# Key norms of a linear-attention mixer: squares as the stationary side, tokens on partitions

## The chip, the cores and the metric

The kernel runs on one core of one Trainium2 chip. The metric is the device time of one execution in microseconds (us); lower is better. The core's engines are named as in the profile: PE is TensorE (matrix products; PEld is its load of the stationary side), DVE is VectorE, ACT is ScalarE, POOL is GpSimd, and SP is SyncE, which here issues nearly all DMAs.

## The reference, cut to what matters

One residual block over 512 tokens of width 1024: a gated feed-forward, a mixer, a second gated feed-forward, each between two normalisations. The mixer has two halves: a delta-rule time mixing with 8 heads of 64 channels, and a causal convolution of width 31 over 512 channels. The change lies in the first half, in the sum over a head's 64 channels of the squared scaled key:

```python
r, k, v = ps[..., :o1], ps[..., o1:o2], ps[..., o2:o3]
...
kk = heads(k * k_k)
kk = kk * lax.rsqrt(jnp.maximum(jnp.sum(kk * kk, axis=-1, keepdims=True), 1e-12))
...
y = rwkv7_recurrence(rh, wh, kh, vh, -kk, kk * ah)
```

Per token t and head, the recurrence updates a state S by S = S (diag(w_t) + z_t^T b_t) + v_t^T k_t, with z_t = -kk_t, b_t = kk_t a_t, and reads y_t = S r_t.

## The kernel before, in words

Inputs, outputs and intermediate results are float32. Large products are made of three passes in a split format: each operand is cut into a high and a low part (`whi`, `wlo` for weights, `hT` for activations), and `mm3` issues high by high (L129), low by high (L132) and high by low (L133). Weights come as blocks of 128 x 1024 by DMA on SP's queue (`wraw`), ACT rounds them to the high part (L105), DVE subtracts to get the low part (L108).

The program runs the first feed-forward (0 to 385 us of the trace), the mixer (385 to 663) and the second feed-forward (663 to 1053). In the mixer the heads are handled as four pairs, two heads of 64 channels on the 128 partitions, 512 tokens along the free dimension. For each pair `prep` makes one projection of 24 matmuls for the key (`psk`), one for `r` and one for `v`, with much in between:

- decay and rate from small up-projections (matmuls L723 and L725), scans and exponentials on DVE and ACT;
- the arrays `bk` (two scaled keys, last written at L747) and `z`;
- the key norm (L751 to L757): ACT squares the scaled key into a tile `sq` (its tag is `tk`), PE sums over channels with two columns of ones (`ind`, a view of the tile `blkones`), ACT copies the sum out of PSUM (L755), and a DMA writes it to the DRAM tensor `nd` (L756);
- the score matrices in `scores`: 16 matmuls L799, 16 L807 and 64 L817 per pair, each 64 partitions deep, with masked copies out of PSUM (`ZT` at L803, `LU` at L823, `E` at L830 or L828);
- the centred values (L778, L779) copied to `SV` by ACT (L780, L781), and the bonus matmul L783, whose PSUM buffer those copies free.

Two pairs make a group. `solve(G)` writes the group's score matrices to DRAM (`md` from `Mt`, L840), reads them back in another layout (`N`, L845, and `D`, the norms from `nd`, L846), takes the reciprocal of `D`, multiplies `N` by it (L853) and solves 31 steps of a triangular system on DVE (L862, L865). Results go out and back through DRAM (`rd`, `td`, into `Mt` and `T`), and `solve_b` takes them up on PE (L903). The tokens of `nd` stand in rows of 64 (pair, chunk of 64 tokens, head, half chunk) with 32 tokens each.

The convolution of a channel block waits for two projections, then makes its padded input `gpad` (L663, DVE); some of its tokens are summed on DVE (L671, L674), the rest by products on ACT (L678, L681) and sums on POOL (L682).

What stands next to what on an engine's queue is not written out: a list scheduler orders every engine's instructions by priorities and by its own model of durations and dependencies. The string `PLAN` and the tables `O_*` and `T_*` set priorities and the tags of PSUM buffers (tags A and B have three buffers each, C has two). A small change in one operation can therefore reorder what follows it on any engine.

Of the kernel before, what the change touches and what calls it, by code (L numbers as in the profile page):

```python
# [18 lines left out]
P = 128  # L19
D = 1024  # L20
SEQ = 512
# [505 lines left out]
T_PR = 'BBBBC'  # L527
# [13 lines left out]
class Mixer:  # L541
# [160 lines left out]
    def prep(self, hp):  # L702
        c, nc, v = self.c, self.c.nc, self.v
        G, l = hp // 2, hp % 2
# [9 lines left out]
        gr = (slice(0, 64), slice(64, 128))  # L714
        for par in range(2):
# [33 lines left out]
        nc.vector.scalar_tensor_tensor(z, ch(k), v["k_k"][:, h1], lam[:, :, 0:64], ALU.mult, ALU.mult)  # L749
        sq = self.t([P, SEQ], "tk", 2)  # L750
        nc.scalar.activation(sq, k, AF.Square, scale=v["k_k"][:, h1])  # L751
        pn = self.ps([2, SEQ], T_PR[1])
        nc.tensor.matmul(pn, lhsT=self.ind, rhs=sq, start=True, stop=True)
        n2 = sq[0:2]
        nc.scalar.copy(n2, pn)  # L755
        nc.sync.dma_start(self.ndram[G].rearrange("(l c h f) i -> l h c (f i)", l=2, c=8, h=2)[l],  # L756
                          n2.rearrange("h (c i) -> h c i", c=8))  # L757
        tc.cur_priority += O_PR[hp] - O_PK[hp]
        psr = self.proj()
        r_ = self.t([P, SEQ], "tk", 2)  # L760
# [559 lines left out]
```

## Time and profile before

| what | us |
|---|---|
| median of 2 runs (1056.44 to 1057.47) | 1056.95 |
| the profiled execution | 1054.72 |
| its span in the trace | 1052.9 |
| PE busy | 1011.4 (96%) |
| DVE busy | 777.1 (74%) |
| ACT busy | 484.8 (46%) |
| POOL busy | 147.0 (14%) |

The profiled execution is one of its own, 1.8 us of it outside the span. Times of views are counted from the span's start. A busy PE is not a PE at its best pace: matmuls overlap in their pipeline, so the pace is read from the distance between starts, not from one row's duration. A float32 matmul outside the split format shows as two passes (x2).

### The profile page before, as it was taken

How to read it: one execution, taken by the hardware profiler on the slowest of the kernel's cores; microseconds unless marked ns; L12 is line 12 of the kernel's file. 1: busy time of each engine (PE TensorE's matmuls, PEld its weight loads, DVE VectorE, ACT ScalarE, POOL GpSimd, SP SyncE). 2: the span in 40 equal slices, each digit the busy share in tenths (PEclk: the TensorE clock that was granted, in tenths of full speed). 3: DMA queues.
4: the chain of work that ended last, by engine and by line, in shares of the span. 5: the costliest groups of instructions: out<-in, count | busy, mean ns of one | idle time of the engine just before them, and what ended most of it. 6: DMA issues, size and time to landing. Idle time of an engine off the chain costs nothing.

```text
span 1052.9 us, 18597 instructions
## 1 busy us (share of the span) xinstructions
PE 1011.4 (96%) x7570; PEld 892.1 (85%) x7570; DVE 777.1 (74%) x1392; ACT 484.8 (46%) x724; POOL 147.0 (14%) x164
## 2 busy tenths in 40 slices
PE   8999999999999899989988898999999999999997
PEld 8899999998888787757667676788999999988885
DVE  5799989985334756789568797687999899853335
ACT  7453444443224435665766375433534444432232
POOL 0000000000000020365788380000000000000000
PEclk9999999999999999999996989999999999999999
DMA  5233333324425221212420310722333333234231
GB/s 200 81 121 104 117 101 107 100 96 145 150 89 185 86 81 62 77 56 80 91 72 22 61 62 5 271 86 82 120 103 118 101 107 100 96 131 144 89 118 80
DMA packets 54589, 107.77 MB, mean 102 GB/s; under 512 B 28776, under 2 KB 28904, under 8 KB 54504
## 3 DMA queue, kind: packets, MB, share of 16 engines
q1 hardware_dynamic: 53640, 103.96, 30.9%
q10 hardware_dynamic: 864, 2.63, 0.7%
q8 instruction: 59, 0.97, 0.4%
q14 instruction: 26, 0.21, 0.1%
HBM read 98.69 MB, written 7.88 MB: 101 GB/s over the span
## 4 chain that ended last, share of the span: by engine, by line
PE 81%; DVE 10%; ACT 3%; DMA 3%; issue 1%; POOL 1%; SPq 0%; DVEq 0%; ACTq 0%; POOLq 0%
PE ps L129 25%; PE ps L133 25%; PE ps L132 25%; DVE ps L674 1%; DVE wlo L108 1%; PE ps L941 1%; PE ps L817 1%; DMA lraw<-w 1%; POOL cacc L682 1%; DMA D<-nd 1%; DVE E L945 1%; ACT cacc L1033 1%; PE ps L194 1%; DVE llo L108 0%; ACT whi L105 0%
## 5 line engine op out<-in xcount | busy, mean ns | idle before, releaser
L108 DVE TENSOR_TENSOR wlo<-wraw,whi 128x1024 fp32r<-128x1024 f32 x103 | 129.2, 1254 | 138.2 <-ACT whi L105 137.8
L129 PE MATMUL ps<-hT,whi 128*128 128x256 f32 (+1 forms) x600 | 196.2, 329 | 1.1 <-ACT hT L179 0.7
L105 ACT CAST whi<-wraw 128x1024 fp32r<-128x1024 f32 x105 | 110.2, 1050 | 184.9 <-PE ps L132 107.5
L133 PE MATMUL ps<-hT,whi 128*128 128x256 f32 (+1 forms) x600 | 194.4, 326 | 0.4 <-DVE hT L186 0.2
L132 PE MATMUL ps<-hT,wlo 128*128 128x256 f32 (+1 forms) x600 | 194.2, 325 | 0.3 <-DVE ms_s L164 0.3
L682 POOL TENSOR_TENSOR cacc<-cacc,cpr 128x512 f32<-128x512 f32 (+2 forms) x120 | 128.6, 1071 | 33.3 <-ACT cpr L681 25.0
L129 PEld LDWEIGHTS ps<-hT,whi 128*128 128x128 f32 x600 | 114.9, 192 | 14.8 <-issue 3.1
L133 PEld LDWEIGHTS ps<-hT,whi 128*128 128x128 f32 x600 | 114.4, 191 | 11.8 <-issue 1.7
L132 PEld LDWEIGHTS ps<-hT,wlo 128*128 128x128 f32 x600 | 115.0, 192 | 10.4 <-issue 1.5
L132 PE MATMUL ps<-whi,gh 128*128 128x512 f32 x288 | 112.0, 389 | 0.0
L133 PE MATMUL ps<-wlo,gh 128*128 128x512 f32 x288 | 112.0, 389 | 0.0
L681 ACT ACTIVATE cpr<-gpad,vecs 128x512 f32<-128x512 f32 (+2 forms) x120 | 71.1, 601 | 37.4 <-POOL cacc L682 37.0
L132 PE MATMUL ps<-tsum,slo 128*128 128x256 f32 x288 | 80.0, 283 | 0.0
L133 PE MATMUL ps<-tsum,shi 128*128 128x256 f32 x288 | 80.0, 283 | 0.0
L129 PE MATMUL ps<-tsum,shi 128*128 128x256 f32 x288 | 76.3, 283 | 0.0
L129 PE MATMUL ps<-whi,gh 128*128 128x512 f32 x288 | 71.5, 389 | 0.0
L133 PEld LDWEIGHTS ps<-wlo,gh 128*128 128x128 f32 x288 | 54.1, 188 | 11.2
L132 PEld LDWEIGHTS ps<-whi,gh 128*128 128x128 f32 x288 | 54.1, 188 | 11.2
L129 PEld LDWEIGHTS ps<-whi,gh 128*128 128x128 f32 x288 | 53.9, 188 | 11.1
L132 PEld LDWEIGHTS ps<-tsum,slo 128*128 128x128 f32 x288 | 55.3, 192 | 0.0
L133 PEld LDWEIGHTS ps<-tsum,shi 128*128 128x128 f32 x288 | 55.3, 192 | 0.0
L365 ACT CAST shi<-s 128x1024 fp32r<-128x1024 f32 x36 | 37.8, 1050 | 36.0 <-DVE s L358 22.1
(273 smaller groups left out, 2328.0 us busy)
## 6 DMA issues: line engine op xcount, KB each, us to landing
wraw<-w SPq DMA_DIRECT2D x105, 512.0 KB, 3.6
lraw<-w SPq DMA_DIRECT2D x57, 512.0 KB, 3.7
x<-x SPq DMA_DIRECT2D x8, 512.0 KB, 4.5
xs<-x SPq DMA_DIRECT2D x8, 512.0 KB, 2.6
x<-xs SPq DMA_DIRECT2D x8, 512.0 KB, 6.3
gain<-gains ACTq DMA_DIRECT2D x5, 512.0 KB, 5.2
out<-x SPq DMA_DIRECT2D x3, 512.0 KB, 2.6
N<-md SPq DMA_DIRECT2D x4, 256.0 KB, 3.6
```

The lines of the kernel that those rows point to most:

```text
L105: c.last_hi = nc.scalar.copy(hi, raw)
L108: c.last_lo = (eng or nc.vector).tensor_tensor(lo, raw, hi, ALU.subtract)
L129: i = nc.tensor.matmul(out, lhsT=lh, rhs=rh, start=start, stop=False)
L132: nc.tensor.matmul(out, lhsT=ll, rhs=rh, start=False, stop=False)
L133: return nc.tensor.matmul(out, lhsT=lh, rhs=rl, start=False, stop=stop)
L194: i = c.nc.tensor.transpose(out=pt[:, k], in_=self.xn[t][:, kk * P : (kk + 1) * P], identity=c.ident)
L365: nc.scalar.copy(sh, sums)
L674: self.dve_queue(nc.vector.scalar_tensor_tensor(dst, gp[:, j : j + n], dw[:, j : j + 1], lo, ALU.mult, ALU.add), False)
L681: nc.scalar.mul(pr, gp[:, n + j : j + SEQ], dw[:, j : j + 1])
L682: self.pool_queue(nc.gpsimd.tensor_tensor(hi, hi, pr, ALU.add), j == 1)
L817: nc.tensor.matmul(ps[s][dst[par], cc, r], lhsT=bk[g, c0 + cc, s], rhs=E[g, l, par, c0 + cc, 1] if r else I2[g], start=True, stop=True)
L941: nc.tensor.matmul(pa[par][:, cc].rearrange("p a b -> p (a b)"), lhsT=Z_[g, d0 + cc].rearrange("p a b -> p (a b)"), rhs=L_[g, d0 + cc].rea ...
```

## The change

Before, the ones are the stationary side (128 x 2) and the squares the moving side (128 x 512), so the sum comes out as 2 partitions (heads) by 512 tokens, and one DMA writes it to `nd` in 16 runs of 64 tokens.

After, each block of 128 tokens of the squares is the stationary side and the two columns of ones move: four matmuls per pair, whose sums come out as 128 partitions (tokens) by 4 blocks by 2 heads. ACT copies them to a new tile `n2` of 128 x 8, and four DMAs write them, one for each half of the partitions (`a`) and head (`h`), with 64 x 4 single elements of 4 bytes each. The content of `nd` is the same.

```diff
         sq = self.t([P, SEQ], "tk", 2)
         nc.scalar.activation(sq, k, AF.Square, scale=v["k_k"][:, h1])
-        pn = self.ps([2, SEQ], T_PR[1])
-        nc.tensor.matmul(pn, lhsT=self.ind, rhs=sq, start=True, stop=True)
-        n2 = sq[0:2]
+        pn = self.ps([P, 4, 2], T_PR[1])
+        for t in range(4):
+            nc.tensor.matmul(pn[:, t], lhsT=sq[:, t * P : t * P + P], rhs=self.ind, start=True, stop=True)
+        n2 = self.t([P, 4, 2], "n2")
         nc.scalar.copy(n2, pn)
-        nc.sync.dma_start(self.ndram[G].rearrange("(l c h f) i -> l h c (f i)", l=2, c=8, h=2)[l],
-                          n2.rearrange("h (c i) -> h c i", c=8))
+        nd = self.ndram[G].rearrange("(l t a h f) i -> l a h (f i) t", l=2, t=4, a=2, h=2)[l]
+        for a in range(2):
+            for h in range(2):
+                nc.sync.dma_start(nd[a, h], n2[gr[a], :, h])
         tc.cur_priority += O_PR[hp] - O_PK[hp]
```

Lines behind L757 have numbers three higher in the changed kernel (L817 is L820 there, L799 is L802, L807 is L810, L783 is L786). The scheduler's order changes on every engine in the mixer. Three places show it.

On PE in the second pair's score matrices (L817, two operands `bk` and `E` or the identity; L129, L132 and L133 are the projections of `hT`), before, up to the next projection after the bonus matmul L783:

```order
L778 MATMUL ps<-cen,v 64x64
L779 MATMUL ps<-cen,v 64x64
L783 MATMUL ps<-tk,blkones 128x512
L817 MATMUL ps<-I_3958,bk 64x64 x2
L817 MATMUL ps<-E,bk 64x64 x2
...
L129 MATMUL ps<-hT,whi 128x512
L132 MATMUL ps<-hT,wlo 128x512
```

and after:

```order
L820 MATMUL ps<-E,bk 64x64
L786 MATMUL ps<-tk,blkones 128x512
L129 MATMUL ps<-hT,whi 128x512
L820 MATMUL ps<-E,bk 64x64
L132 MATMUL ps<-hT,wlo 128x512
L820 MATMUL ps<-I_3958,bk 64x64
L133 MATMUL ps<-hT,whi 128x512
```

The score matmuls, which stood in rows without a projection matmul between them, now stand singly between projection matmuls, and the bonus matmul stands among them.

On PE in the third pair, at its scores L799 and L807 (L802 and L810 after; `z` by `bk` and by the identity), before:

```order
L133 MATMUL ps<-hT,whi 128x512
L129 MATMUL ps<-hT,whi 128x512
L799 MATMUL ps<-bk,z 64x128 x16
L807 MATMUL ps<-I_3958,z 64x64 x16
L132 MATMUL ps<-hT,wlo 128x512
```

and after (from the first L802):

```order
L802 MATMUL ps<-bk,z 64x128 x9
L129 MATMUL ps<-hT,whi 128x512
L802 MATMUL ps<-bk,z 64x128 x2
L132 MATMUL ps<-hT,wlo 128x512
L802 MATMUL ps<-bk,z 64x128
...
L810 MATMUL ps<-I_3958,z 64x64
L129 MATMUL ps<-hT,whi 128x512
L810 MATMUL ps<-I_3958,z 64x64
L132 MATMUL ps<-hT,wlo 128x512
```

The two rows of 16 become one run of nine and many of one or two, each between two projection matmuls.

On DVE at the first solve's start (`D` and `N` are the solve's norms and matrices, `gpad` and the rows of L671 and L674 the convolution, `ZT`, `LU` and `E` masked copies of the second pair's scores), before:

```order
L847 TENSOR_SCALAR D<-D 128x32
L663 SCALAR_TENSOR_TENSOR gpad<-cpr,ps 128x512
L848 RECIPROCAL D<-D 128x32
L671 TENSOR_SCALAR ps<-gpad,vecs 128x320
L108 TENSOR_TENSOR wlo<-wraw,whi 128x1024
L851 TENSOR_SCALAR D<-D 64x16 x2
...
L674 SCALAR_TENSOR_TENSOR ps<-gpad,vecs,ps 128x320 x9
L853 TENSOR_TENSOR N<-N,D 128x1024
L855 MEMSET ps 128x512
L674 SCALAR_TENSOR_TENSOR ps<-gpad,vecs,ps 128x320
L823 TENSOR_TENSOR LU<-ps,mask_3967 128x512
L830 TENSOR_TENSOR E<-ps,mask_3967 64x512 x2
```

and after:

```order
L850 TENSOR_SCALAR D<-D 128x32
L851 RECIPROCAL D<-D 128x32
L854 TENSOR_SCALAR D<-D 64x16 x2
L826 TENSOR_TENSOR LU<-ps,mask_3967 128x512
L833 TENSOR_TENSOR E<-ps,mask_3967 64x512 x2
L856 TENSOR_TENSOR N<-N,D 128x1024
L663 SCALAR_TENSOR_TENSOR gpad<-cpr,ps 128x512
L671 TENSOR_SCALAR ps<-gpad,vecs 128x320
```

The masked copies `LU` and `E`, which stood behind the product with `N`, now stand ahead of it, and the convolution's `gpad`, which stood ahead of it, now stands behind it.

## Rows read from the trace of the kernel before

**Rows 1.** The page's chain that ended last, shares of the span by engine.

```profile
PE 81%; DVE 10%; ACT 3%; DMA 3%; issue 1%; POOL 1%; SPq 0%; DVEq 0%; ACTq 0%; POOLq 0%
```

**Rows 2.** Stretches: us, busy PE PEld DVE ACT POOL, PEclk, DMA share, GB/s.

```profile
431.40:463.00 31.60, 28.34 (x303) 21.40 (x302) 23.29 (x48) 19.72 (x42) 19.99 (x28) 0.95 0.29 77
472.50:513.90 41.40, 41.40 (x332) 28.42 (x331) 31.80 (x79) 21.77 (x32) 24.77 (x20) 1.00 0.31 78
513.90:524.80 10.90, 9.77 (x94) 7.14 (x94) 7.87 (x8) 10.41 (x17) 8.92 (x9) 0.84 0.52 117
552.30:601.90 49.60, 43.37 (x402) 35.51 (x404) 40.80 (x123) 22.81 (x34) 30.95 (x23) 0.79 0.22 41
601.90:663.00 61.10, 54.64 (x646) 43.81 (x647) 50.77 (x136) 40.34 (x76) 25.65 (x33) 0.92 0.15 47
```

**Rows 3.** Waits of PE in 385 to 663: us in total, times, longest.

```profile
PE ps L817 <- DVE LU L823: 2.2, 1, 2.2
PE ps L799 <- DVE bk L747: 2.0, 1, 2.0
...
PE ps L778 <- DVE E L830: 1.1, 1, 1.1
```

**Rows 4.** PE's timeline, first solve: start, us, line, tile, [idle before <-releaser].

```profile
516.41 1.31 PE L903 MATMUL ps<-Mt 32*32 32x32 f32 x62 [1.00 <-DMA Mt<-rd]
```

**Rows 5.** PE's timeline: a key norm, and transposes early in the program.

```profile
431.40 1.02 PE L753 MATMUL ps<-tk,blkones 128*2 128x512 f32 x2
432.35 0.50 PE L129 MATMUL ps<-hT,whi 128*128 128x512 f32 x1
...
25.35 1.03 PE L194 MATMUL ps<-ident,xn 128*128 128x128 f32 x8
```

**Rows 6.** PE's timeline: projection matmuls in a row, then L817 in a row.

```profile
439.14 0.39 PE L132 MATMUL ps<-hT,wlo 128*128 128x512 f32 x1
...
443.47 0.39 PE L133 MATMUL ps<-hT,whi 128*128 128x512 f32 x1
443.79 0.34 PE L817 MATMUL ps<-I,bk 64*64 64x64 f32 x8
...
445.80 0.50 PE L129 MATMUL ps<-hT,whi 128*128 128x512 f32 x1
```

**Rows 7.** The chain in order of time, 430 to 452: start, us, what.

```profile
432.46 0.58 ACT tk L755
...
433.06 1.21 DMA nd<-tk
...
434.92 2.50 DMA D<-nd
...
441.91 3.64 DMA md<-Mt
...
446.13 4.71 DMA N<-md
```

**Rows 8.** SP's timeline at the second pair's key norm: start, us of issue.

```profile
433.06 0.26 SPq L756 DMA_DIRECT2D nd<-tk  x1
```

**Rows 9.** DMA issues: count, KB each, median us to landing.

```profile
td<-T SPq DMA_DIRECT2D x4, 128.0 KB, 3.7
```

**Rows 10.** PE's timeline in the third pair: single L817 between projection matmuls.

```profile
503.10 0.32 PE L817 MATMUL ps<-I,bk 64*64 64x64 f32 x2
503.35 0.50 PE L132 MATMUL ps<-hT,wlo 128*128 128x512 f32 x1
503.78 0.33 PE L817 MATMUL ps<-I,bk 64*64 64x64 f32 x2
```

**Rows 11.** ACT's timeline: a convolution step, a copy of centred values.

```profile
444.05 0.46 ACT L681 ACTIVATE cpr<-gpad,vecs 128x192 f32<-128x192 f32 x1 [0.22 <-POOL cacc L682]
...
458.92 0.58 ACT L780 COPY SV<-ps 64x512 f32<-64x512 f32 x1
```

## The prediction

> **What bounds the kernel now.** I read the chain of waits first: 81% of it is TensorE's own work [rows 1], so what counts is what changes on TensorE, or makes it wait. I then cut the mixer, where the edit lies, into stretches bounded by TensorE's own landmarks [rows 2]: from the key-norm matmul (L753) of the second head pair to the first decay matmul (L723) of the third (431.4 to 463.0), from the third pair's L753 to the fourth's L723 (472.5 to 513.9), from there to the fourth pair's L753 (to 524.8), and two late stretches. In 472.5 to 513.9 TensorE is busy for 41.40 of 41.40 us: every 0.1 us added to its stream there is paid in full. In 431.4 to 463.0 it is idle for 3.26 us. Two waits make these up, 2.2 and 1.1 us [rows 3], both on VectorE results that stand in its queue behind the load of N. The granted clock of 0.95 over 31.6 us means another 1.6 us lost to half clock after those waits. The same reading gives 1.0 us of waiting and 0.16 x 10.9 = 1.7 us of half clock around the first block solve (L903), in 513.9 to 524.8 [rows 2, 4]. After 552.3 TensorE idles for 6.2 and 6.5 us and loses about 15 us more to the half clock; that part is a chain of small dependent steps.
>
> **The edit itself.** Per head pair one float32 matmul with 2 stationary and 512 moving columns goes. It runs as two passes: from its start at 431.40 to the next projection matmul at 432.35 it takes 0.95 us [rows 5]. Four matmuls with 128 stationary and 2 moving columns come, eight passes in all. No row has such a shape. From below nothing goes under a handful of small matmuls: eight passes of L817 take 0.17 us in a batch (2.01 us for 48 instructions of two passes [rows 6]). From above stands a row of eight transposes with the same 128 stationary columns, but 128 moving ones: 1.03 us [rows 5]. I take 0.9, since loading 128 columns eight times is what the two shapes share: four pairs change by -0.2 us together, between -3.1 and +0.3. The copy out of PSUM shrinks from 512 to 8 elements per partition; its 0.58 us [rows 7] lies on ScalarE, which is not late there: nothing. One DMA becomes four on SyncE's queue, 0.26 us of issue each [rows 8]: 12 x 0.26 = 3.1 us over the kernel, behind which the next weight load, the read-back of D, the writes of the score matrices and the load of N are queued. Weight blocks are loaded a block or two ahead and absorb 0.8 us; for the first solve D and N come 0.8 us later than they would.
>
> Each of the four now writes 256 separate 4-byte pieces where the old one wrote 16 runs of 256 bytes, which landed in 1.21 us [rows 7]. The nearest row with many small pieces is the write of T: 2048 runs of 64 bytes, 3.7 us [rows 9]. I take 2.5 us from the last issue, between 1.2 and 3.7: D would be ready at about 439.5 instead of 437.4. The Trainium skill speaks against such a layout: "DMA: Bandwidth & Descriptors", in its rules for kernel authors, says that a strided last dimension becomes one descriptor per element, and under Specifications that pieces under 512 B cost a read-modify-write. The trace agrees on the direction only: it has no 4-byte piece, and 2048 pieces of 64 bytes in 3.7 us are no disaster.
>
> **What the edit moves.** The scheduler orders each engine by its own model of the program, and a small change in one operation reshuffles everything behind it. From the second pair's key norm on TensorE's order differs, and this is the main term. In the second pair, 48 of 64 L817 matmuls stood in one run. Now more than half stand singly between projection matmuls (L129, L132, L133). In the third pair the same happens to seven L799 and fifteen L807 and to most L817. I counted runs of small matmuls between projection matmuls, in the order of each engine: 4 become 23 from the second pair's key norm to the third pair's L723, 2 stay 2 up to the third pair's key norm, 25 become 66 up to the fourth pair's L723, and 1 stays 1 up to its key norm. That is 60 more runs, nearly all of one instruction; the number of projection matmuls (231 over the four) is the same.
>
> The trace of before has such an alternation in the third pair. A single L817 starts at 503.10 and the next at 503.78: 0.68 us for it and one projection matmul [rows 10]. Apart, a projection matmul takes 0.228 us (19 steps from 439.14 to 443.47) and an L817 2.01 / 48 = 0.042 us [rows 6]. So a switch there and back costs 0.68 - 0.27 = 0.41 us, and **60 switches cost 24.6 us**, on the engine that sets the end. The clock granted in that stretch was 1.00, so this is a full-clock price [rows 2].
>
> Against it stand the waits. In the second pair VectorE now does the masked copies (LU, E) before it waits for N, so the 4.9 us of waiting and half clock there go. But the convolution's first step (gpad, L663) now stands behind N on VectorE; ScalarE's convolution starts behind gpad, and five of its steps stand ahead of the copies of SV (L780, L781), which release the PSUM buffer that the bonus matmul (L783) needs. N is loaded after D (2.50 us), then md (3.64), then N itself (4.71) [rows 7]; with scores copied some 2 us sooner, N lands at about 447.5, not 450.9. Five steps at 0.46 + 0.22 us and two copies of 0.58 us [rows 11] and some 2.5 us for the three instructions ahead of them bring L783 to about 454.5. By the unit prices above TensorE is there at about 449: a new wait of some 5 us in the place of the old 4.9. Net 0, between -5 and +2. L903 moves into the third pair's matmuls, behind which its data should have landed: -1.0 - 1.7 = **-2.7 us**, if the first solve isn't late. VectorE waits inside that solve for a weight block whose buffer TensorE frees later than now, so I count its data some 7 us later (an own estimate): at 523.4 instead of 516.41 [rows 4]. By the unit prices above TensorE reaches L903 only near 526, a cover of some 3 us.
>
> The fourth pair starts with the same wait of 2.0 us for bk (L747) [rows 3] and takes as long as before. In the late stretches the second solve's steps go earlier and fewer output-projection matmuls are left for the end (48 for 65 after the last group of L992: 17 x 0.228 = 3.9 us), while the last convolution's projection stands behind L903 and a copy that waits for a DMA: I take **-2 us**, between -6 and +4.
>
> Sum: 24.6 - 0.2 + 0 - 2.7 - 2 = **+20 us**. The profiled execution took 1054.72 us (span 1052.9), 2.2 us under the median of 1056.95; on it the sum gives 1074.7, on the median 1077, 1.9% slower.
>
> **Rivals.** (a) The late stretches absorb it. They hold 12.7 us of idle time and 15 us of lost clock [rows 2]; were the fourth pair and the convolutions not the ones that set their start, up to half of the 24.6 would vanish: +8 us, 1065. Against it: nearly all that follows depends on the fourth pair's scores or on convolutions which move with the stream. (b) The 4-byte pieces land late. If D came 5 us later than counted for both solves, VectorE would hold LU and E behind it, and TensorE would wait for their PSUM buffers: +10, 1087. It decides from about 2 us of delay, where the masked copies are late for the 49th L817. (c) The clock falls in the long alternation (some 45 us, 66 switches). In the old one of about 17 us it stayed at full [rows 2], which speaks against it; at half clock each projection matmul takes 0.228 us more: 66 x 0.228 = +15 on top, 1092. (d) On the other side, faster: single matmuls between projections cost no more than in a row. Then 24.6 falls away, and the waits at L903 and the shorter end leave -5 us: 1052. It turns on the pair period: it must stay under some 0.35 us for the sum to fall below zero. [...] The rows of the alternation say 0.41 us more, and I go by them.
>
> **How the numbers follow.** Forecast 0.63 (1077, itself good to about 8 either way: the bounds of wait, solve and late stretches), (a) 0.15, (b) 0.09, (c) 0.08, (d) 0.05. The range 1062 to 1092 leaves out (d), the low part of (a) and the high parts of (b) and (c), under 0.2 in all. A measurement of this kernel can tell about 2% from no change, that is 1036 and 1078. The forecast lies just inside: slower by over 2% gets 0.44 of its 0.63, hence 0.28, plus (b) and (c): 0.45; within 2% 0.53; faster 0.02.
>
> **What would show it.** In the changed kernel: pairs of a projection matmul and a single L817 (there L820), L799 or L807 at a period of about 0.68 us through most of the second and third pair; TensorE with few idle us there but the fourth pair's key norm some 22 us later than at 524.8; the bonus matmul of the second pair waiting for ScalarE's copies; L903 without a wait; four writes of nd landing within 4 us; and the mixer's end 20 us later. A period under 0.4 us, a fourth pair that starts on time, or a mixer whose late stretches shrink by over 10 us would prove me wrong.

## The result, and the profile after

The changed kernel takes **1124.57 us** (two runs, 1123.07 and 1126.08) for 1056.95 before: a ratio of 1.0653, 95% interval 1.0606 to 1.0701, so 6.5% slower. The forecast was 1077, between 1062 and 1092: the direction was right, the size was not. The profiled execution took 1126.08 us, its span is 1124.3.

The chain that ended last, by engine, differs by a point here and there from before [rows 1]: DMA, issue and SyncE's queue grew by one each, TensorE and VectorE fell by one:

```profile
PE 80%; DVE 9%; DMA 4%; ACT 3%; issue 2%; POOL 1%; SPq 1%; DVEq 0%; ACTq 0%; POOLq 0%
```

The stretches of after between the landmarks of [rows 2] (second pair's key norm to third pair's first decay matmul, third key norm to fourth decay matmul, from there to the fourth key norm; the fourth line runs from the first combine matmul (L935, L932 in before), which multiplies `ZT` by a solve's result, to the first matmul of the second feed-forward, for which before took 118.61 us). Columns: us, busy time of PE, PEld, DVE, ACT, POOL, granted clock, DMA share, GB/s:

```profile
435.06:481.59 46.53, 37.50 (x274) 23.25 (x272) 24.19 (x59) 14.77 (x32) 14.74 (x23) 0.66 0.24 41
495.69:561.37 65.68, 65.68 (x427) 40.66 (x426) 29.21 (x68) 23.97 (x37) 23.60 (x21) 1.00 0.29 64
561.37:572.69 11.32, 8.32 (x30) 6.06 (x29) 9.18 (x9) 8.71 (x14) 7.24 (x7) 0.85 0.20 69
614.89:739.40 124.51, 106.28 (x1072) 86.95 (x1072) 92.10 (x261) 65.32 (x115) 56.75 (x56) 0.81 0.20 53
```

The second of these is pure TensorE work, busy from end to end at full clock, and 24.3 us longer than its 41.40 of before: that is the alternation, as forecast, with 25 more projection matmuls and L903 in the stretch. The first is something else: 9.03 us idle, and a clock of 0.66 where it was 0.95. The last is 5.9 us longer, mostly idle time. The longest waits of after (total, times, longest), of TensorE and of VectorE, say what for; they answer to [rows 3]:

```profile
PE ps L820 <- DVE LU L826: 14.4, 2, 8.2
```

```profile
DVE D L850 <- DMA D<-nd: 26.2, 2, 14.7
```

VectorE waits for `D`, with the masked copies (LU, E) queued behind it, and TensorE waits for these copies' PSUM buffers. The chain of after in order of time (start, us, what) goes on from there to the writes of `nd`; it answers to [rows 7, 8]:

```profile
436.24 0.58 SPq L760
436.87 0.61 SPq L760
437.52 0.61 SPq L760
438.18 9.19 DMA nd<-n
447.53 0.50 SPq L849
448.07 4.42 DMA D<-nd
```

One write of 1.21 us has become three issues of 0.6 us each on the path and 9.19 us behind the last of them, and the read of `D` takes 4.42 us for 2.50. So `D` is there at 452.5, not at 437.4: 17.4 us behind the key norm for 6.0 (the key norm itself comes 3.7 us later than in before), and the first scores wait. For the second solve, where the writes of `nd` are issued between those of the score matrices, the same chain holds 14.31 us:

```profile
579.38 14.31 DMA nd<-n
593.75 0.49 SPq L849
594.29 2.46 DMA D<-nd
596.76 0.18 DVE D L850
```

What the first wait does to the clock is seen in TensorE's timeline and the stretches behind it (columns as above):

```profile
454.24 0.48 PE L820 MATMUL ps<-I,bk 64*64 64x64 f32 x4 [8.20 <-DVE LU L826]
```

```profile
445.00:450.00 5.00, 1.04 (x13) 0.59 (x9) 0.00 (x0) 1.44 (x2) 0.00 (x0) 0.95 0.63 79
450.00:455.00 5.00, 0.69 (x8) 0.50 (x8) 2.33 (x7) 0.00 (x0) 0.00 (x0) 0.50 0.41 64
...
480.00:485.00 5.00, 5.00 (x9) 2.41 (x9) 3.45 (x8) 3.00 (x5) 1.18 (x1) 0.50 0.00 0
485.00:490.00 5.00, 5.00 (x15) 3.18 (x14) 3.34 (x8) 2.05 (x5) 4.12 (x5) 0.79 0.33 107
490.00:495.00 5.00, 5.00 (x23) 4.13 (x22) 4.42 (x8) 4.12 (x7) 1.93 (x3) 1.00 0.01 3
```

The granted clock falls to 0.50 (1.2 GHz) in the wait and stays there until 487, through 27 us (from 460) in which TensorE is busy without a gap, most of them in the alternating order. An alternation of one projection matmul and L820s costs 1.13 us there (two pieces of the chain):

```profile
459.79 0.41 PE ps L820 x4
460.20 0.72 PE ps L129
```

At full clock, in the third pair, the same kind of pair has nearly the period of before's [rows 10], 0.69 us for 0.68:

```profile
510.83 0.33 PE L810 MATMUL ps<-I,z 64*64 64x64 f32 x2
511.09 0.50 PE L129 MATMUL ps<-hT,whi 128*128 128x512 f32 x1
511.52 0.32 PE L810 MATMUL ps<-I,z 64*64 64x64 f32 x2
```

The edited matmuls themselves, for [rows 5]: four of them, eight passes, and the next projection matmul 0.81 us after the first.

```profile
435.06 0.95 PE L754 MATMUL ps<-blkones,tk 128*128 128x2 f32 x8
435.87 0.48 PE L129 MATMUL ps<-hT,whi 128*128 128x512 f32 x1
```

### The profile page after: what moved, and what is told of

It is laid out like the page before. It is cut to its first block, busy times and chain, and to the rows that moved or that the text cites. A ratio compares the mean times of both kernels' runs of the same rounds, so it can differ in the third digit from the quotient of the medians.

```text
span 1124.3 us, 18651 instructions
## 1 busy us (share of the span) xinstructions
PE 1059.6 (94%) x7594; PEld 920.4 (82%) x7594; DVE 776.5 (69%) x1392; ACT 484.0 (43%) x724; POOL 144.9 (13%) x164
## 3 DMA queue, kind: packets, MB, share of 16 engines
q1 hardware_dynamic: 57920, 103.96, 30.2%
## 4 chain that ended last, share of the span: by engine, by line
PE 80%; DVE 9%; DMA 4%; ACT 3%; issue 2%; POOL 1%; SPq 1%; DVEq 0%; ACTq 0%; POOLq 0%
PE ps L129 25%; PE ps L132 24%; PE ps L133 24%; DMA nd<-n 2%; PE ps L820 2%; POOL cacc L682 1%; DVE ps L674 1%; PE ps L944 1%; DMA D<-nd 1%; DVE wlo L108 1%; ACT cpr L681 1%; DVE E L948 1%; DMA N<-md 1%; PE ps L194 1%; PE ps L802 0%
## 5 line engine op out<-in xcount | busy, mean ns | idle before, releaser
L129 PE MATMUL ps<-hT,whi 128*128 128x256 f32 (+1 forms) x600 | 203.2, 340 | 4.5 <-DVE k L502 3.3
L132 PE MATMUL ps<-hT,wlo 128*128 128x256 f32 (+1 forms) x600 | 201.5, 337 | 0.3 <-DVE ms_s L164 0.3
L133 PE MATMUL ps<-hT,whi 128*128 128x256 f32 (+1 forms) x600 | 199.9, 335 | 0.4 <-DVE hT L186 0.2
L129 PEld LDWEIGHTS ps<-hT,whi 128*128 128x128 f32 x600 | 117.2, 195 | 22.3 <-issue 5.6
L132 PEld LDWEIGHTS ps<-hT,wlo 128*128 128x128 f32 x600 | 117.4, 196 | 11.1 <-issue 1.1
L133 PEld LDWEIGHTS ps<-hT,whi 128*128 128x128 f32 x600 | 117.0, 196 | 11.4 <-DVE hT L186 0.4
L132 PE MATMUL ps<-whi,gh 128*128 128x512 f32 x288 | 112.0, 389 | 0.0
L133 PE MATMUL ps<-wlo,gh 128*128 128x512 f32 x288 | 112.0, 389 | 0.0
L132 PE MATMUL ps<-tsum,slo 128*128 128x256 f32 x288 | 80.0, 283 | 0.0
L133 PE MATMUL ps<-tsum,shi 128*128 128x256 f32 x288 | 80.0, 283 | 0.0
L129 PE MATMUL ps<-tsum,shi 128*128 128x256 f32 x288 | 76.3, 283 | 0.0
L129 PE MATMUL ps<-whi,gh 128*128 128x512 f32 x288 | 71.5, 389 | 0.0
L132 PEld LDWEIGHTS ps<-whi,gh 128*128 128x128 f32 x288 | 54.1, 188 | 11.2
L133 PEld LDWEIGHTS ps<-wlo,gh 128*128 128x128 f32 x288 | 54.1, 188 | 11.2
L129 PEld LDWEIGHTS ps<-whi,gh 128*128 128x128 f32 x288 | 53.9, 188 | 11.1
L132 PEld LDWEIGHTS ps<-tsum,slo 128*128 128x128 f32 x288 | 55.3, 192 | 0.0
L133 PEld LDWEIGHTS ps<-tsum,shi 128*128 128x128 f32 x288 | 55.3, 192 | 0.0
```

The costliest lines, as they stand in the source:

```text
L129: i = nc.tensor.matmul(out, lhsT=lh, rhs=rh, start=start, stop=False)
L132: nc.tensor.matmul(out, lhsT=ll, rhs=rh, start=False, stop=False)
L133: return nc.tensor.matmul(out, lhsT=lh, rhs=rl, start=False, stop=stop)
```

## The experiments

Two things changed at once: the edit (matmuls, copy, writes) and the order of every engine's queue. To tell them apart, an order can be held: a table names for each engine the order of its instructions, and each is tied to the one ahead of it, with no wait between engines added. The edit of a kernel with a held order is this, and the order is a matter of the table alone (line numbers are 47 to 53 higher in these kernels):

```diff
+ORDER = (
...
+def pin(c):
...
+        for a, b in zip(out, out[1:]):
+            c.tc.add_manual_dep(b, a.name, mybir.DependencyInfo(mybir.DependencyClass.NoSync, mybir.DependencyReason.DATA), reason="order")
```

The table sums up all runs; ratios are to before on the same chip, with their 95% interval. Below, "old" is before's order or edit, "new" the changed kernel's. The four kernels named runs16, runs8 and runs32 put the norms at other places of `nd` than the solve reads them from: they time a write and are no replacement.

| kernel | us | ratio to before |
|---|---|---|
| changed kernel | 1124.57 | 1.0653 (1.0606 to 1.0701) |
| new_edit_old_order | 1074.07 | 1.0173 (1.0150 to 1.0197) |
| old_edit_new_order | 1098.66 | 1.0410 (1.0357 to 1.0463) |
| runs16_new_order | 1103.24 | 1.0456 (1.0433 to 1.0478) |
| runs16_old_order | 1060.02 | 1.0046 (1.0030 to 1.0063) |
| runs32_old_order | 1055.33 | 0.9999 (0.9984 to 1.0014) |
| runs8_old_order | 1064.41 | 1.0074 (1.0052 to 1.0097) |
| old_edit_new_order_batched | 1078.21 | 1.0211 (1.0179 to 1.0243) |
| old_edit_old_order_batched | 1052.52 | 0.9968 (0.9956 to 0.9981) |
| new_edit_new_order_d_late | 1110.35 | 1.0518 (1.0481 to 1.0556) |
| new_order_to_pair4_then_old | 1089.63 | 1.0309 (1.0263 to 1.0356) |
| old_order_to_pair4_then_new | 1069.75 | 1.0132 (1.0104 to 1.0161) |
| old_edit_batched_n_late | 1049.63 | 0.9934 (0.9918 to 0.9950) |
| old_new_second_solve_behind | 1074.28 | 1.0154 (1.0116 to 1.0191) |
| new_batched_second_solve_behind | 1082.27 | 1.0248 (1.0222 to 1.0273) |
| old_new_n_load_ahead | 1063.46 | 1.0072 (1.0044 to 1.0100) |
| new_batched_n_load_ahead | 1074.02 | 1.0158 (1.0137 to 1.0178) |

### The edit without the order, and the order without the edit

new_edit_old_order is the changed kernel with before's order held; the four matmuls and the four writes stand where the one of each stood.

> The changed kernel's code (four small matmuls, copy of 8 columns, four DMAs of 4-byte pieces), but every engine's queue is held in the order of the kernel before. Theory A (the pieces land late: in the changed kernel the four writes take 9.19 us to land where the old one took 1.21, D comes at 452.5 instead of 437.4, and VectorE and the reads behind it on SyncE's queue wait): the loss shows here too, as N follows D on both queues; TensorE's 2.19 us wait for LU grows by some 7 us in each of the two solves, with half clock behind it: 1070 to 1095 us. Theory B (the order makes the loss, the pieces have slack): within 5 us of the kernel before, 1052 to 1062. Theory C (both, and each needs the other, since only in the new order LU stands behind D): also near 1057 to 1065.

old_edit_new_order is before with the changed kernel's order held.

> The kernel before (one matmul with two stationary columns, one DMA of 16 runs), but every engine's queue is held in the order of the changed kernel. Theory A (late pieces make most of the loss): only the alternation of single small matmuls and projection matmuls is left, 60 more switches at 0.41 us less some waits that go: about 1077 us, 1068 to 1086. Theory B (the order makes the loss): 1105 to 1125. Theory C (interaction): 1065 to 1085, and the loss of 67 is more than the sum of both single losses.

Measured: +18 us and +43 us over before's 1055.9, so the order alone costs more than the whole forecast, and the edit alone, forecast at nothing, costs over a quarter of what the change does. The two together cost 68, some 7 more than the sum, of which the spread of 11 us among the runs of old_edit_new_order may be a part. 1098.66 us lies in none of the three ranges written down for it: the order costs more than its 60 switches and less than the whole loss. In old_edit_new_order's trace the stretch from the third key norm to the fourth decay matmul is that of after, busy throughout at full clock, and the bonus matmul (L831 there) waits for `SV`, as forecast:

```profile
477.26:543.09 65.83, 65.83 (x422) 39.97 (x421) 32.00 (x72) 25.97 (x40) 23.62 (x22) 1.00 0.27 65
```

```profile
455.47 2.08 PE L831 MATMUL ps<-tk,blkones 128*128 128x512 f32 x2 [4.85 <-ACT SV L829]
```

### How small the pieces are

The writes of the key norms alone are changed, in four steps: one DMA of 128 runs of 32 bytes, four of 64 runs of 16 bytes, four of 128 runs of 8 bytes, and the changed kernel's four of 256 runs of 4 bytes.

```diff
-                nc.sync.dma_start(nd[a, h], n2[gr[a], :, h])
+                nc.sync.dma_start(nd[a, h], n2[gr[a], 2 * h : 2 * h + 2].rearrange("p t h -> p (t h)"))
```

(runs16; `nd` is viewed accordingly.) With the changed kernel's own order:

> The changed kernel, but each of the four DMAs writes the same 256 elements as 64 runs of 16 bytes, so the norms stand at wrong places of nd (the outputs differ for that reason); every queue's order is that of the changed kernel. Theory A: the writes land in 1.2 to 4 us, D comes before 443 us, TensorE's wait of 8.2 us for LU goes and with it the half clock from 450 to 487: 1068 to 1088 us, near the old edit in the new order. Theory B: no more than 8 us better than the changed kernel, 1115 to 1125. What else would speak for A: the stop of PE and ACT at 413 to 415 us in the first pair goes too.

With before's order held:

> Four small matmuls, copy of 8 columns and four DMAs of 64 runs of 16 bytes (norms at wrong places), every queue held in the order of the kernel before. What is left of the change is the matmuls, the copy and three more DMA issues per pair. My forecast for these parts was -0.2 us of matmuls and nothing for the copy and the issues: 1054 to 1062 us by all theories; over 1065 would mean that the matmuls or the issues cost something by themselves.

The same with 8 bytes, and with 32 bytes in one DMA:

```diff
-                nc.sync.dma_start(nd[a, h], n2[gr[a], :, h])
+                i = nc.sync.dma_start(nd[a, h], n2[gr[a], 2 * h : 2 * h + 2])
```

> Four DMAs of 128 runs of 8 bytes per pair (norms at wrong places of nd), old order. Landing behind the last issue was 1.40 us with one DMA of 128 runs, 2.93 us with 4 x 64 runs of 16 bytes, 8.37 with 4 x 256 runs of 4 bytes. Theory A (the number of runs sets it): 512 runs land in 4.5 to 5.5 us, and the time lies between 1060 and 1074, some 1065. Theory B (runs below some size are slow whatever their number): 8 to 9 us, 1072 to 1075.

```diff
-        for a in range(2):
-            for h in range(2):
-                nc.sync.dma_start(nd[a, h], n2[gr[a], :, h])
+        nc.sync.dma_start(self.ndram[G].rearrange("(l s) (e i) -> l (s e) i", l=2, i=8)[l], n2.rearrange("p t h -> p (t h)"))
```

> Four small matmuls and the copy of 8 columns, but one DMA of 128 runs of 32 bytes (norms at wrong places of nd), all queues in the order of the kernel before. Four DMAs of 16-byte runs in this order gave 1060.02 us. Theory A (the extra 4 us are three more issues of some 0.6 us each, behind which D, md and N are late): 1053 to 1058, same as before. Theory B (the matmuls or the copy cost them): 1058 to 1062.

Measured, in before's order: 1055.33, 1060.02, 1064.41, 1074.07 us for 32, 16, 8 and 4 bytes, and 1055.75 for the old edit. So the matmuls and the copy cost and bring nothing, three more issues with 16-byte pieces cost 4 us, and 4-byte pieces another 14; in the new order (1098.66, 1103.24, 1124.57) they cost 4.6 and another 21.3. (1103.24 lies between the two ranges written down; `D` was there in time and the stop in the first pair went, as the first theory had it, but the order underneath costs more than that theory allowed.) The chain in order of time shows why, in one row each of runs32, runs16, runs8 and new_edit_old_order: what lies behind the last issue of the second pair's writes.

```profile
432.85 1.40 DMA nd<-n
```

```profile
434.11 2.93 DMA nd<-n
```

```profile
435.77 4.58 DMA nd<-n
```

```profile
439.50 8.37 DMA nd<-n
```

All write 4 KB. With the 1.21 us of 16 runs [rows 7] that makes 16, 128, 256, 512 and 1024 runs in 1.21, 1.40, 2.93, 4.58 and 8.37 us: by these rows some 7 ns for each run more ((8.37 - 1.21) / 1008). They are one place of the program; the medians over all 16 writes of runs16_old_order, runs8_old_order and new_edit_old_order (count, KB, us from issue to landing) are

```profile
nd<-n SPq DMA_DIRECT2D x16, 1.0 KB, 1.9
nd<-n SPq DMA_DIRECT2D x16, 1.0 KB, 3.7
nd<-n SPq DMA_DIRECT2D x16, 1.0 KB, 8.8
```

so the steps are 7 and 10 ns for each run more, (3.7 - 1.9) / 256 and (8.8 - 3.7) / 512. As every variant writes the same bytes, the count of runs and their size change together, and these rows can't tell one from the other.

### The alternation

old_edit_new_order_batched is old_edit_new_order with the small matmuls of the second and third pair held back until eight are pending. In the order between those key norms and the decay matmuls behind them, runs of small matmuls fall from 23 to 6 and from 66 to 12. On PE's queue (P a projection matmul, s a small one), at one place:

```diff
-P s P s P s P s P s P s P s P s
+P P P P P P P P s s s s s s s s
```

> The kernel before in the changed kernel's order, with one difference: on TensorE, between the second pair's key norm and the fourth pair's first decay matmul, single small matmuls are held back until eight are pending and then issued in a row. The runs of small matmuls between projection matmuls fall from 23 to 6 and from 66 to 12. Theory A (a switch there and back costs 0.41 us at full clock): 71 switches less are 29 us, so about 1070 us against the 1098.66 of the same order without it, 1062 to 1080. Theory B (the switches are cheap, the order costs by the places of the convolution and of the solve's instructions on VectorE, ScalarE and GpSimd): 1092 to 1104.

Measured: 20.5 us less, of 29 for all 71 switches; the second pair gains 3 us only (29.72 us for 32.75, of which it idles 7.52 for 4.85). From the third key norm to the fourth decay matmul it is 49.83 us for 65.83, of which it now idles 3.19 and loses 0.07 x 49.83 = 3.5 to the clock (an estimate from the granted clock of 0.93); (16.0 + 3.2 + 3.5) / 54 = 0.42 us per run. The same in before's own order, where 25 runs of the third pair become 8:

> The kernel before in its own order, but on TensorE single small matmuls are held back until eight are pending, in the same stretch as above: runs of small matmuls fall from 25 to 8 in the third pair and stay at 4 in the second. Theory A (0.41 us a switch): 17 less are 7 us, 1045 to 1052 us, faster than both kernels. Theory B (switches are cheap): 1054 to 1059.

1052.52, 3.2 us faster than before and half a microsecond outside the range of the theory. The stretch shrinks by 5.7 us, of which it now idles 1.4: (5.7 + 1.4) / 17 = 0.42 us per run. 2.2 us come back in the next stretch, where TensorE idles 3.2 us for 1.1. The price of a switch holds in an order with no other change.

### The late D

new_edit_new_order_d_late is the changed kernel in its order, with one move on DVE's queue, in both solves:

```diff
-L850 TENSOR_SCALAR D<-D
-L851 RECIPROCAL D<-D
-L854 TENSOR_SCALAR D<-D x2
 L826 TENSOR_TENSOR LU<-ps,mask
 L833 TENSOR_TENSOR E<-ps,mask x2
+L850 TENSOR_SCALAR D<-D
+L851 RECIPROCAL D<-D
+L854 TENSOR_SCALAR D<-D x2
 L856 TENSOR_TENSOR N<-N,D
```

> The changed kernel with one difference: on VectorE the four instructions on D (L850, L851, L854) stand right ahead of the product with N instead of ahead of the masked copies LU and E, in both solves. Theory A (late pieces cost because LU and E queue behind D): TensorE's waits of 8.20 and 6.22 us for LU fall under 2 us and most of the half clock behind the first goes: 1100 to 1112 us against 1124.57. Theory B (N and the solve are late too, and what waits for them costs as much): 1118 to 1127.

Measured: 14.2 us less than the changed kernel, most of it at the second solve (42.20 us from the fourth key norm to the first combine matmul become 30.85). At the first solve nothing is gained, 46.46 us for 46.53: the masked copies come early, but `N`, loaded behind `D`, and the convolution's `gpad` behind `N`, are as late as ever, and the bonus matmul (L838 here) waits for `SV` in the place of L820's wait for `LU`:

```profile
458.10 1.23 DVE L908 TENSOR_TENSOR N<-N,D 128x1024 f32<-128x1024 f32 x1 [7.41 <-DMA N<-md]
```

```profile
465.75 2.08 PE L838 MATMUL ps<-tk,blkones 128*128 128x512 f32 x2 [6.43 <-ACT SV L836]
```

### Where the order costs: two halves

Two kernels with the old edit take one order up to the fourth pair's key norm and the other behind it.

> The kernel before; all queues in the changed kernel's order up to the fourth pair's key norm, from there in the order before (the same instructions lie ahead of that point in both orders but for one on VectorE, ScalarE and GpSimd). In the trace of the old edit in the new order, 28.3 us came up to that point and 9.3 us of the mixer behind it. Theory A (the two losses are separate, the second made by the order of the late part itself, the last convolution's projection standing behind the second solve's L903): 1080 to 1088 us. Theory B (the late loss is an echo of the early one, through the second convolution on GpSimd that begins later): 1089 to 1098.

> The kernel before; all queues in the order before up to the fourth pair's key norm, from there in the changed kernel's order. Theory A: the late part's own order costs its 9.3 us here too: 1062 to 1068 us. Theory B: 1052 to 1059.

Measured: +32.9 and +13.1 us; their sum, 46, is the 42.7 of the whole order within its spread. By its time the first kernel falls into the rival's range, by 0.6 us, and the second lies 1.8 us above the theory's. The trace of the first decides: behind the fourth key norm it has 27.73 and 119.49 us up to and from the first combine matmul, before 27.51 and 118.61, so there is no echo, and its whole loss lies ahead. The losses are separate, then: the late part does not absorb what the third pair loses, and adds its own. (The orders with a late second pair scatter: old_edit_new_order ran between 1093 and 1104 us. From the second key norm to the third decay matmul one such trace has 32.75 us at a clock of 0.90, another 37.28 at 0.78, over the same wait of 4.8. The order on TensorE is the same there: in old_edit_new_order the clock is back at 1.00 from 459, 3.4 us behind the wait and amid the alternation, in new_order_to_pair4_then_old it stays at 0.50 until 470. Five us of each, in that order:)

```profile
460.00:465.00 5.00, 5.00 (x23) 3.01 (x23) 4.96 (x14) 3.38 (x8) 4.37 (x9) 1.00 0.00 0
460.00:465.00 5.00, 5.00 (x15) 2.51 (x14) 2.73 (x8) 3.41 (x8) 4.45 (x8) 0.50 0.00 0
```

### What is lost behind the fourth key norm

In old_order_to_pair4_then_new the last convolution starts 91.4 us behind the fourth key norm, for 81.4 in before. Two things in the order could do it. First, the second solve's first group on TensorE (L903) and ScalarE's copies around it stand ahead of the last projection; they are put back behind it: L903 behind the 23 projection matmuls that followed it, and on ACT:

```diff
-L887 COPY T1p<-T x2
 L979 ACTIVATE ps<-ps
 L105 CAST whi<-wraw
-L905 COPY P1<-ps x2
+L887 COPY T1p<-T x2
 L660 ACTIVATE cpr<-ps
 L105 CAST whi<-wraw
+L905 COPY P1<-ps x2
```

> The edit is undone. The order is that of old_order_to_pair4_then_new (before's up to the fourth key norm, the changed kernel's behind it), with one piece put back as before had it: the second block solve's first group (32 matmuls of L903) behind the 23 projection matmuls that stand behind it, and on ScalarE the four copies that belong to it (T1p of L887, two of L905) behind the weight conversion of the last projection block and behind the last convolution's tanh, where before had them. The kernel without that piece took 1069.75 us; its ScalarE waited 11.35 us for the read of T in front of the weight conversion (77.4 us behind the fourth key norm), and its last convolution began 91.4 us behind that key norm, 10 us later than in before. Theory (the place of the solve holds up the last projection): the tanh comes some 7 to 8 us earlier, the last convolution begins near 83 to 84, the stretch from the first combine matmul to the second feed-forward stage falls from 124.0 to about 118 to 119, and the time is 1062 to 1065; what is left above before (6 to 9 us) lies between the fourth key norm and the first combine matmul. Rival (the solve's end is what counts): the solve's steps come 7 us later and hold up the combine by as much as the convolution gains: 1068 to 1071.

> The edit is undone. The order is that of old_edit_new_order_batched (the changed kernel's order with small matmuls held until eight are pending; 1078.21 us), with the same piece put back as in old_new_second_solve_behind. Theory (the place of the solve holds up the last projection): its last convolution began 89 us behind the fourth key norm; it begins near 82 now, the stretch from the first combine matmul to the second feed-forward stage falls from 126.5 to about 119, and the time is 1070 to 1073. Rival (the solve's end is what counts): 1077 to 1080.

Measured: 1074.28 (1069.75 without the move) and 1082.27 (1078.21): not faster; the intervals overlap, and both times lie above the rival's ranges too. That theory fell: the place of the solve's first group is not what costs (the move was not tried together with the one below). The second question was what makes the solve itself late. In the kernel without the move `N`'s load stands on SyncE's queue behind two weight blocks, and VectorE waits for it (SyncE's queue, then VectorE; N's product is L901 here):

```profile
552.38 5.23 SPq L122 DMA_DIRECT2D wraw<-w  x2
557.78 1.09 SPq L893 DMA_DIRECT2D N<-md  x2
```

```profile
564.43 1.29 DVE L901 TENSOR_TENSOR N<-N,D 128x1024 f32<-128x1024 f32 x1 [5.76 <-DMA N<-md]
```

One move, on SP alone:

```diff
 L846 D<-nd x2
 L74 wraw<-w
-L74 wraw<-w
 L845 N<-md x2
+L74 wraw<-w
```

> The edit is undone. The order is that of old_order_to_pair4_then_new (1069.75 us) with two instructions moved: on SyncE's queue the second solve's load of N (two DMAs of L845) goes ahead of the second of the two weight blocks that stood in front of it; before had one block in front of it. In the kernel without the move that block was issued at 31.3 us behind the fourth key norm, N's load at 31.8, and VectorE's product with N (L853) came at 38.4 after 5.76 us of waiting for it; in before the load was issued at 23.3 and the product came at 30.2 with no wait. The buffer of N is free here at about 28.1, when the first solve's last matmuls end. Theory (the second solve is late because its N stands behind a weight block): the load is issued at 28 to 28.5, the product comes near 33, the second solve and all that hangs on it 5 to 6 us earlier: 1063 to 1066. Rival (the wait for the third convolution's last sum, 5.2 us at the combine matmul, sets the start of all that follows): 1068 to 1071.

> The edit is undone. The order is that of old_edit_new_order_batched (1078.21 us) with the same move of N's load as in old_new_n_load_ahead. In the kernel without the move the load was issued at 27.4 us behind the fourth key norm and the product came at 34.0 after 5.72 us of waiting. Theory (N stands behind a weight block): the load is issued near 24, the product comes near 29 to 30, 1073 to 1075. Rival (the convolution's last sum): 1077 to 1079.

The same rows of old_new_n_load_ahead:

```profile
550.21 0.36 SPq L122 DMA_DIRECT2D wraw<-w  x1
551.92 1.08 SPq L893 DMA_DIRECT2D N<-md  x2
555.11 0.33 SPq L122 DMA_DIRECT2D wraw<-w  x1
```

```profile
556.97 2.04 DVE L901 TENSOR_TENSOR N<-N,D 128x1024 f32<-128x1024 f32 x1 [0.47 <-DMA N<-md]
```

Behind the fourth key norm (525.98 and 522.81) the load goes from 31.8 to 29.1 us and the product from 38.4 to 34.2; the wait is gone. The stretch from the first combine matmul to the second feed-forward falls from 124.02 to 119.44 us (before 118.61), the time from 1069.75 to 1063.46; in the batched order from 126.54 to 122.16 and from 1078.21 to 1074.02. So the order's late loss is half a load that stands one place too far back. The other half lies between the fourth key norm and the first combine matmul, 34.28 us for 27.51, where TensorE waits 5.2 us for the third convolution's last sum (2.65 in before); that was read from the traces and not tried, so this half has no shown cause.

### A version that beats both

old_edit_batched_n_late is before, its order held, with the third pair's small matmuls in batches and, on DVE, the first solve's product with `N` moved behind half of the masked copies that stood behind it:

```diff
-L853 TENSOR_TENSOR N<-N,D
-L855 MEMSET ps
 L674 SCALAR_TENSOR_TENSOR ps<-gpad,vecs,ps
 L823 TENSOR_TENSOR LU<-ps,mask
 L830 TENSOR_TENSOR E<-ps,mask x2
+L853 TENSOR_TENSOR N<-N,D
+L855 MEMSET ps
```

> The kernel before in its own order with single small matmuls held back until eight are pending (that alone gave 1052.52 us), and on VectorE, in the first solve, the product with N behind the first half of the masked copies LU and E instead of ahead of them. Theory A (TensorE's waits of 2.24 and 0.87 us for LU and E and the half clock behind them, together some 5 us, come from N standing ahead): 1045 to 1050 us. Theory B (another wait takes their place, ScalarE's SV copies or the solve's end, which is 2 us later): 1051 to 1055.

1049.63 us, ratio 0.9934 (0.9918 to 0.9950): the smallest time of all, 0.7% under before. The stretch of the 3.26 idle us of [rows 2], 31.56 us from key norm to decay matmul, takes 27.93.

## Why the prediction was wrong

**What bounds it.** Right: TensorE's stream, and every 0.1 us added to it in the third pair was paid in full.

**The edit on TensorE.** Right: 0.9 us was taken for the four matmuls, 0.81 measured, for 0.95 before, and the whole kernel with the new matmuls, the copy and one DMA is at 0.9999 of before.

**The main term, the switches.** Right in mechanism and size. From the third key norm to the fourth decay matmul the order puts 41 more runs, 25 more projection matmuls and L903: 41 x 0.41 + 25 x 0.228 + 1.3 = 23.8 us by the forecast's prices, measured 24.5 in old_edit_new_order. From the second key norm to the third decay matmul 19 more runs and 34 fewer projection matmuls are 7.8 - 7.8 = 0; measured +1.2. From the second to the fourth key norm the old edit in the new order is 28.3 us longer (121.63 for 93.36) in its profiled execution, the shortest of four; 24.6 was the term for the switches, and some 22 the forecast up to there. Most of what is over is the gain at L903 that didn't come (below). The wait for `SV` that was to replace the old waits of the second pair came, 4.85 us where 5 was written.

**The step that failed: the four writes.** "I take 2.5 us from the last issue, between 1.2 and 3.7: D would be ready at about 439.5 instead of 437.4." It was 9.19 us, and `D` came at 452.5; counted from the key norm, 17.4 us for 8.1. The upper bound was the write of T, 2048 runs of 64 bytes in 3.7 us [rows 9], which looked like the worse case; the writes of `nd` cost some 7 ns a run, at which T's would have taken 14. So the number of runs alone is not the rule, and what makes T's cheaper was not tried. The DMA records of after say where the time is not: the 4-byte packets of the second pair's four writes have all started by 440, and the landing is at 447.4; the weight block issued behind them at 438.90 moves its 128 packets from 441.7 to 450.4, where the one behind before's write takes 3.6 us from issue to landing. What holds them is not shown. The issues were 0.6 us each, not 0.26 [rows 8]. Together: 4.6 us for three more issues and 16-byte pieces, 21.3 for 4-byte ones, 25.9 of the 68 in the new order, 18 in the old. They take the place of the wait for `SV`: the second pair's stretch in after is 46.53 us for old_edit_new_order's 32.75, 9.03 idle for 4.85, and the other 9.6 us the same matmuls at half clock (the old edit can lose some of it too: 37.28 us in the other trace above); at the second solve 42.20 us for 29.27 up to the first combine matmul.

The Trainium skill, "DMA: Bandwidth & Descriptors", rules for kernel authors, has a strided last dimension lower to one descriptor per element. The forecast called the trace's evidence no disaster and went by T; that rule was the better guide. The DMA lines of before's and after's profile agree with it: 4280 more packets under 512 bytes, where one per element makes 4 x (1024 - 16) = 4032.

```profile
DMA packets 54589, 107.77 MB, mean 102 GB/s; under 512 B 28776, under 2 KB 28904, under 8 KB 54504
```

```profile
DMA packets 58869, 107.77 MB, mean 96 GB/s; under 512 B 33056, under 2 KB 33184, under 8 KB 58784
```

**The second step that failed: the late stretches, at -2 us (-6 to +4).** The order alone costs 13.1 us there. That "the second solve's steps go earlier" was read from their place among the others on TensorE's queue; in fact its product with `N` comes 8 us later (38.4 for 30.2 us behind the fourth key norm), since on SyncE's queue the load stands behind one more weight block. Moving that load gave back 6.3 us; the other half is open. The forecast's own suspicion, the last projection behind L903 and a copy that waits for a DMA, is the piece whose undoing gained nothing.

**L903, at -2.7.** The wait of [rows 4] went, but the fourth pair then waits for the key instead, in after as in old_edit_new_order, and the stretch gains no time (11.32 and 11.40 us for 10.86):

```profile
565.50 0.75 PE L129 MATMUL ps<-hT,whi 128*128 128x512 f32 x1 [3.00 <-DVE k L502]
```

**The rivals.** (b), late pieces, was the right mechanism: VectorE held LU and E behind `D`, TensorE waited for their buffers, in both solves. It was priced at 10 us for 5 us of delay and given 0.09; the delay was 13 us at the first solve (9.3 counted from the key norm), and the price with the issues 25.9. In the kernel with the late `D` the hold is gone in both solves, and only the second gains: at the first, `N` is as late. (c), a clock that falls in the alternation, did not happen: 65 us of it ran at 1.00. What happened is that a clock which a wait had brought down stayed down through it, 37.6 us in after; in old_edit_new_order it rose again within 7. (a) fell: the late stretches absorbed nothing. (d) fell with the period of 0.69 us. The table of the Trainium skill ("TensorE: Matmul & The Clock Gate", Back-to-back issue gap) has about 60 cycles for up to 64 columns, for a matmul by itself; it has no row for small matmuls between large ones, where the runs here have 0.41 us more for each switch.

The sum as it should have been, from the runs: about 28 up to the fourth key norm by the order, 13 behind it, 26 for the writes: 67, for 67.6 measured. The 26 is itself the difference of two medians, so what this tests is the split of the order's 42.7 into 28 and 13, within a spread of 11 us among that kernel's four runs.

**Open.** In the first pair TensorE and ScalarE stop for some 3 us around 413 to 415 (from that key norm to the next decay matmul 19.79 us for 16.06). A stop is there in all three kernels with 4-byte pieces (18.96 to 19.79 us) and in none with 8, 16 or 32; the trace names no releaser that explains it. The second feed-forward takes 1 to 3 us longer in many of these kernels (384.9 in after, 382.1 in before), which no run separates.

## What to carry to other kernels

Price a DMA by pieces of its own size: a transfer of more runs, each sixteen times as long, was no upper bound. Where the result sits across partitions, one DMA of 32 contiguous bytes from each cost nothing here, while 4-byte pieces cost 18 us; a reader laid out to match those 32 bytes was not built, so its price is open. When a scheduler reorders, read every queue for each load that a later step needs, SyncE's above all: one weight block ahead of one load was worth 6 us. Small matmuls of another shape belong in batches between large ones, at 0.41 us for every switch there and back.

## What was not expected of the hardware

- The landing of a 4 KB write grew with its runs: 1.21, 1.40, 2.93, 4.58, 8.37 us for 16, 128, 256, 512, 1024 at the second pair. The read-back at the first solve took 2.50 us in before and 4.42 in after, but at the second 4.37 and 2.46, so no growth is shown there.
- The issue on SyncE's queue of a write with 256 runs took 0.6 us, that of 16 runs 0.26; in runs16_old_order those of 64 runs took 0.45 for the first of four and 0.59 for those behind it, so the count of runs is not all of it.
- The granted clock, once at 0.50, stayed there in after for 27 us of unbroken work, most of it alternating small and large matmuls, and rose behind a row of projection matmuls with two decay matmuls; in old_edit_new_order it rose amid the alternation, 3.4 us behind the wait. The same alternation entered at full clock kept it for 65 us. What decides is not shown.
